# Decoding from the old states in the heads, and updating the states under the feed-forward network

## The chip, the cores and the metric

One core of one Trainium2 chip runs the whole step. The metric is the device time of one execution in microseconds; lower is better.

## The reference

One inference step of a one-layer decoder with two parallel branches, mLSTM ("m") and retention ("r"), four heads each, key and value width 256, model width 1024. A prompt of 528 tokens (16 meta tokens and 512) and eight running sequences with one new token each go through the same weights. All data are float32. Per head and branch, for each of the eight sequences (decoding):

```
mLSTM:      C_new = w_c * C + w_s * k v^T        h ~ q . C_new   (also n_new, and a denominator)
retention:  S_new = gamma * S + k v^T / 16       o ~ q . S_new
```

Then a norm per head, gates, an output projection, a layer norm, a SwiGLU feed-forward network (width 2816) and a second layer norm. Outputs are the prompt's and the sequences' activations, the prompt's final states, and the updated states C, n, m, S of the eight sequences. C and S of all sequences and heads are 64 blocks of 256 x 256 floats, 256 KB each; every block is read, and every updated block written.

## The kernel before, in words

**The main stream.** All large products go through TensorE in three passes each (high x low, low x high, high x high part of a float32 split in two float32r numbers). Weights come in 154 units of 128 x 1024 (512 KB), loaded from `wall` by SP into three `raw` buffers (`load_units`, L157), split by ACT into `wH` and by DVE into `wL` (`split_units`, L164; three buffers each). `run_step` (L193) runs one unit: 8 contraction steps of 6 matmuls with 260 or 268 columns. In its middle it splits the unit two ahead and loads the one five ahead (`prep`, L189). PSUM of the main stream (`pp`) has two buffers; a unit's result is evacuated while the next unit runs.

**The quarters.** Every two contraction steps (12 matmuls) `run_step` calls `tick`, which resumes generators that stopped at a `yield`, and then `side(i)`. A unit so has four quarters. In the heads' stage, 4 heads x 20 units, `sched` holds for each quarter 0 to 79 of a head (higher numbers run on into the next head) the side work due there: transposes, scores, value products, rotary embedding, norms, decoding. It is written out by hand in L966 to L1062. Engines work through their own queues in program order, so a side operation that waits holds back everything behind it on its engine, weight splits and evacuations too. Side products on TensorE use PSUM tiles `aux` and `acc`, two buffers each.

**Decoding before.** `dec_rows` (L814, at quarter 27 for m, 54 for r) transposes the eight sequences' q and k columns (L818), and POOL writes them to DRAM as 32 rows `kq` of 128 (L823). For each sequence `dec_load` (L832) has SP load the state block into `dC` (three buffers, L835) and one sequence's k and q rows, broadcast over all partitions in four pieces of 512 bytes, into `dkq` (three buffers, L838). `dec_unit` (L841) does this: two products k times v on ACT, a quarter later the new state on DVE, its store by POOL (L850), and two products of q with the new state, summed, on DVE:

```
act(t[:, et, :], k[:, 256:512], AF.Copy, scale=d["vs" + br][:, et, b:b + 1])
...
stt(c, c, w, t.rearrange("p a b -> p (a b)"), ALU.mult, ALU.add)
G.dma_start(o["dC" if br == "m" else "dS"][h, :, b, :], c)
...
stt(t[:, et, :], c[:, et * 256:(et + 1) * 256], 1.0, k[:, 0:256], ALU.mult, ALU.mult,
```

The units of a branch are due at the quarters in `DEC` (L976), their loads up to five quarters earlier. `dec_stat1` (L855, DVE: `pk`), `dec_stat2` (L872, a product with `ones` on TensorE, L877) and `dec_stat3` (L897) make the norm of the result, at 60, 62, 65 for m, 87, 89, 92 for r (the next head's 7, 9, 12), and 79, 82, 85 for r of the last head. `merge_a`, `merge_b` and `last_dec` use it.

**After the heads.** The output projection runs as eight `run_pair` calls (L220: two units, one half of 260 tokens), its first inputs reloaded into `mg`. The feed-forward network starts with four pairs for each token half (L1306 to L1313, eight units whose splits are kept), then 18 x 2 units (L1315), then the down projection (L1336, six columns of three units, then the last two columns in pairs). Side work: evacuations, weight splits, the first layer norm's second half during the first four pairs; POOL is idle from 695 us on until the last layer norm. `kv_load` (L670) reloads saved operands of one head's prompt state before the down projection, for products at the very end.

Of the kernel before, what the change touches and what calls it, by code (L numbers as in the profile page):

```python
# [19 lines left out]
T = 528  # L20
NB = 8
# [56 lines left out]
def body(nc, tc, a, o):  # L78
# [65 lines left out]
    onesR = const.tile([128, 2], F32R, name="onesR")  # L144
    nhalf = const.tile([128, 8], F32, name="nhalf")
# [121 lines left out]
    dsc = keep.tile([128, 3, H, NB], F32, name="dsc")  # L267
# [252 lines left out]

    def dcols(h, sec, r):
        d = tiles[h]
        br = sec[0]
        if sec[1] == "v":
            d["dc" + br] = sm.tile([128, 3, 2, NB], F32, name="dc")
        V.tensor_copy(d["dc" + br][:, "qkv".index(sec[1])], r[:, :, T:])
# [286 lines left out]

    def dec_rows(h, br):  # L814
        d = tiles[h]
        dc = d["dc" + br]
        ps = aux()
        PE.transpose(ps[:32, :128], dc[:, 0:2].rearrange("p s t b -> p (s t b)"), ident)  # L818
        t = wt("tmp", [128, NT], 3)[:32, :128]
        act(t, ps[:32, :128])  # L820
        kq = dram.tile([32, 128], F32, name="kq%d%s" % (h, br))
        d["kq" + br] = kq
        G.dma_start(kq, t)  # L823
        vs = sm.tile([128, 2, NB], F32, name="vs")
        if br == "m":
            tt(vs, dc[:, 2], dsc[:, 1, h:h + 1, :].to_broadcast([128, 2, NB]), ALU.mult, G)
        else:
            G.tensor_scalar(vs, dc[:, 2], 1.0 / 16, None, op0=ALU.mult)
        d["vs" + br] = vs
        d["y" + br] = sm.tile([128, 2, NB], F32, name="y")  # L830

    def dec_load(h, br, b):  # L832
        d = tiles[h]
        c = lt("dC", [128, 512], 3)
        SP.dma_start(c, a["sC" if br == "m" else "sS"][h, :, b, :])  # L835
        k = lt("dkq", [128, 512], 3)
        row = d["kq" + br].rearrange("(s b) c -> b s c", b=NB)[b:b + 1]
        SP.dma_start(k.rearrange("p (s c) -> p s c", s=4), row.broadcast_to([128, 4, 128]))  # L838
        d["dC" + br, b] = (c, k)

    def dec_unit(h, br, b):  # L841
        d = tiles[h]
        c, k = d["dC" + br, b]
# [4 lines left out]
        w = dsc[:, 0, h, b:b + 1] if br == "m" else float(GAMMA[h])  # L848
        stt(c, c, w, t.rearrange("p a b -> p (a b)"), ALU.mult, ALU.add)
        G.dma_start(o["dC" if br == "m" else "dS"][h, :, b, :], c)  # L850
        for et in range(2):
# [741 lines left out]
```

## Time and profile before

| | us |
|---|---|
| median of 3 runs (lowest, highest) | 1065.99 (1061.45, 1079.36) |
| the profiled execution's own time | 1068.46 |
| its span, first to last instruction | 1066.8 |
| heads' stage, to the last projection matmul | about 615 |
| matmuls of the 18 x 2 units of the network | 714 to 921 |
| down projection from | 921 |

Busy shares of the span: PE 97%, PE's weight loads 96%, DVE 56%, ACT 44%, POOL 17%. PE is TensorE, DVE VectorE, ACT ScalarE, POOL GpSimd, SP the engine that issues most loads. A row of the page's last part names an instruction group as line, engine, operation, output <- inputs. The granted clock is a share of TensorE's full 2.4 GHz.

### The profile page before, as it was taken

The numbers are of one execution on the slowest core, as the hardware profiler recorded it, in microseconds if no ns is written. First come the engines' busy times: TensorE is split into PE (matmuls) and PEld (weight loads), VectorE is DVE, ScalarE is ACT, GpSimd is POOL, SyncE is SP. The second block draws the span as 40 slices with busy tenths as digits, with TensorE's granted clock in tenths as the row PEclk, the third lists the DMA queues.
The fourth block names the chain that finished last, engine by engine and source line by source line (L and its number), as shares of the span: only waits on it lengthen the run. The fifth ranks groups of instructions, "written<-read, shape, count | busy, mean of one in ns | idle before, by whom it ended". The sixth has DMA issues, their size and how long they took to land.

```text
span 1066.8 us, 21079 instructions
## 1 busy us (share of the span) xinstructions
PE 1038.9 (97%) x8526; PEld 1028.3 (96%) x8526; DVE 595.4 (56%) x1236; ACT 467.2 (44%) x922; POOL 182.5 (17%) x313
## 2 busy tenths in 40 slices
PE   9999999999999999999998899999999999999996
PEld 8999998999999999999998899999999999999995
DVE  4748764568755487654596566734344343333435
ACT  5555553665544665545564434522222222222213
POOL 1223222322311232221122224200000000000003
PEclk9999999999999999999999899999999999999998
DMA  7254564555663645652456592212222222522302
GB/s 233 94 172 144 191 213 167 176 182 167 199 213 103 209 156 196 219 186 99 152 165 200 194 314 85 81 43 97 99 84 96 99 80 100 184 100 99 139 2 91
DMA packets 86249, 155.31 MB, mean 146 GB/s; under 512 B 8388, under 2 KB 49412, under 8 KB 85896
## 3 DMA queue, kind: packets, MB, share of 16 engines
q1 hardware_dynamic: 76904, 129.41, 36.9%
q0 software_dynamic: 9248, 24.56, 6.5%
q8 instruction: 67, 1.10, 0.4%
q14 instruction: 30, 0.25, 0.1%
HBM read 127.04 MB, written 25.58 MB: 143 GB/s over the span
## 4 chain that ended last, share of the span: by engine, by line
PE 71%; DMA 11%; DVE 8%; issue 5%; ACT 2%; POOL 1%; SPq 1%; ACTq 0%; DVEq 0%; POOLq 0%
PE pp L213 52%; PE pp L236 9%; DMA dkq<-kq3r 3%; DVE dC L100 1%; DMA dS<-dC 1%; PE aux L577 1%; DVE wL L97 1%; PE acc L177 1%; PE acc L178 1%; PE acc L179 1%; DVE dt L100 1%; DMA dkq<-kq0r 1%; DMA dkq<-kq2r 1%; PE pp L344 1%; DMA kq2r<-tmp 1%
## 5 line engine op out<-in xcount | busy, mean ns | idle before, releaser
L213 PE MATMUL pp<-xH,wL 128*128 128x260 f32 (+1 forms) x1248 | 262.9, 292 | 3.9 <-DVE sg L100 3.3
L213 PE MATMUL pp<-xL,wH 128*128 128x260 f32 (+1 forms) x1248 | 255.3, 286 | 0.0
L213 PE MATMUL pp<-xH,wH 128*128 128x260 f32 (+1 forms) x1248 | 254.9, 286 | 0.0
L97 DVE TENSOR_TENSOR wL<-raw,wH 128x1024 fp32r<-128x1024 f32 (+1 forms) x149 | 184.2, 1236 | 95.5 <-ACT wH L94 93.7
L213 PEld LDWEIGHTS pp<-xH,wL 128*128 128x128 f32 x1248 | 195.1, 191 | 5.5 <-DVE sg L100 3.8
L213 PEld LDWEIGHTS pp<-xH,wH 128*128 128x128 f32 x1248 | 195.7, 191 | 0.0
L213 PEld LDWEIGHTS pp<-xL,wH 128*128 128x128 f32 x1248 | 195.6, 191 | 0.0
L94 ACT ACTIVATE wH<-raw 128x1024 fp32r<-128x1024 f32 (+1 forms) x149 | 151.1, 1016 | 73.2 <-PE pp L213 58.3
L213 PE MATMUL pp<-x1H,wH 128*128 128x260 f32 x576 | 116.1, 283 | 0.0
L213 PE MATMUL pp<-x1L,wH 128*128 128x260 f32 x576 | 115.9, 283 | 0.0
L213 PE MATMUL pp<-x1H,wL 128*128 128x260 f32 x576 | 115.9, 282 | 0.0
L97 DVE TENSOR_TENSOR gt<-gt,pp 128x520 f32<-128x520 f32 (+1 forms) x52 | 31.8, 612 | 116.7 <-ACT gt L94 64.1
L213 PEld LDWEIGHTS pp<-x1H,wL 128*128 128x128 f32 x576 | 88.8, 188 | 0.0
L213 PEld LDWEIGHTS pp<-x1H,wH 128*128 128x128 f32 x576 | 88.8, 188 | 0.0
L213 PEld LDWEIGHTS pp<-x1L,wH 128*128 128x128 f32 x576 | 88.5, 188 | 0.0
L94 ACT ACTIVATE dt<-dkq,vs 128x256 f32<-128x256 f32 x128 | 57.8, 500 | 65.7 <-DMA dkq<-kq3r 21.8
L97 POOL TENSOR_TENSOR sq<-sq 128x260 f32<-128x260 f32 x12 | 9.2, 764 | 351.3 <-ACT sq L94 350.7
L94 ACT ACTIVATE hH<-gt 128x520 fp32r<-128x520 f32 (+1 forms) x26 | 14.9, 571 | 96.9 <-DVE gt L97 96.9
L213 PE MATMUL pp<-hH,wL 128*128 128x260 f32 x264 | 53.2, 283 | 0.0
L213 PE MATMUL pp<-hH,wH 128*128 128x260 f32 x264 | 53.1, 282 | 0.0
L213 PE MATMUL pp<-hL,wH 128*128 128x260 f32 x264 | 53.0, 282 | 0.0
L94 ACT ACTIVATE gt<-pp 128x520 f32<-128x520 f32 (+2 forms) x28 | 14.7, 526 | 81.9 <-PE pp L213 62.4
(371 smaller groups left out, 1927.9 us busy)
## 6 DMA issues: line engine op xcount, KB each, us to landing
raw<-wall SPq DMA_DIRECT2D x154, 512.0 KB, 3.5
dC<-sC SPq DMA_DIRECT2D x32, 256.0 KB, 4.9
dC<-dC POOLq DMA_DIRECT2D x32, 256.0 KB, 4.0
dC<-sS SPq DMA_DIRECT2D x32, 256.0 KB, 4.3
dS<-dC POOLq DMA_DIRECT2D x32, 256.0 KB, 4.0
raw<-xT SPq DMA_DIRECT2D x8, 268.0 KB, 4.6
mg<-mgd SPq DMA_DIRECT2D x8, 260.0 KB, 5.4
z<-xT SPq DMA_DIRECT2D x8, 260.0 KB, 6.4
```

The source lines that it names most:

```text
L94: A.activation(out, in_, func, **kw)
L97: (eng or V).tensor_tensor(out, x, y, op=op)
L100: V.scalar_tensor_tensor(out, x, s, y, op0=op0, op1=op1, **kw)
L177: PE.matmul(out, ll, rh, start=start, stop=False)
L178: PE.matmul(out, lh, rl, start=False, stop=False)
L179: PE.matmul(out, lh, rh, start=False, stop=stop)
L213: PE.matmul(ps[:, hi, :wd], w, r[:, lo:lo + wd], start=(st.first and i == 0 and pi == 0), stop=(st.last and i == n - 1 and pi == 2))
L236: PE.matmul(ps[:, hi, :n], w[:, c], r, start=(i == 0 and pi == 0), stop=(i == last and pi == 2))
L344: PE.matmul(first_ps[u][:, hi, :268], w[:, c], r[:, k, hi * 268:(hi + 1) * 268], start=(k == 0 and pi == 0), stop=(k == 7 and pi == 2))
L577: PE.transpose(ps[:m, i * 256 + dt * 128:i * 256 + dt * 128 + 128], src[:, dt, 128 * j:128 * j + m], ident)
```

## The change

Decoding no longer computes q . C_new from the updated block. It uses q . C_new = w_c (q . C) + w_s (q . k) v: two DVE products per block on the old state, and one small correction per branch, with q . k summed over partitions by a product with `ones` on TensorE. The rows go to DRAM as four rows of 1024, so that one broadcast load brings q for four sequences. The updated blocks are made again later: from the second token half of the network's first pairs on, POOL loads every block a second time (five buffers `uC`) with k rows for two sequences (`uk`), ACT and DVE compute the update, POOL stores it. `upd_at` starts an update every 13/4 quarters. `dsc` moves from pool `keep` to `const`, where `vsA` keeps the scaled v of all heads. Due times of decoding move, `kv_load` moves to the sixth down-projection column, and the SBUF space kept for POOL's DMA descriptors is set to 8192 bytes per partition.

```
+    dsc = const.tile([128, 3, H, NB], F32, name="dsc")
+    vsA = const.tile([128, 2 * H, 2, NB], F32, name="vsA")
...
+    kqd = {}
     def dec_rows(h, br):
         d = tiles[h]
         dc = d["dc" + br]
+        kp = sm.tile([128, NB, 2], F32, name="kp")
+        ks = sm.tile([128, NB], F32, name="ks")
+        tt(kp, dc[:, 0], dc[:, 1], ALU.mult, G)
+        tt(ks, kp[:, :, 0], kp[:, :, 1], ALU.add, G)
+        vs = vsA[:, 2 * h + (br == "r")]
+        v = dcol(h, br, 2)
+        if br == "m":
+            tt(vs, v, dsc[:, 1, h:h + 1, :].to_broadcast([128, 2, NB]), ALU.mult, G)
+        else:
+            G.tensor_scalar(vs, v, 1.0 / 16, None, op0=ALU.mult)
+        yield
         ps = aux()
-        PE.transpose(ps[:32, :128], dc[:, 0:2].rearrange("p s t b -> p (s t b)"), ident)
+        PE.transpose(ps[:32, :128], dc[:, 0:2].rearrange("p s b t -> p (s b t)"), ident)
+        PE.matmul(ps[:, 128:128 + NB], ones, ks, start=True, stop=True)
         t = wt("tmp", [128, NT], 3)[:32, :128]
         act(t, ps[:32, :128])
-        kq = dram.tile([32, 128], F32, name="kq%d%s" % (h, br))
-        G.dma_start(kq, t)
+        kq = dram.tile([4, 1024], F32, name="kq%d%s" % (h, br))
+        kqd[h, br] = kq
+        G.dma_start(kq.rearrange("a (r c) -> (a r) c", c=128), t)
+        vk = sm.tile([128, 2, NB], F32, name="vk")
+        tt(vk, vs, ps[:, 128:128 + NB]....to_broadcast([128, 2, NB]), ALU.mult)
...
     def dec_load(h, br, b):
         d = tiles[h]
-        c = lt("dC", [128, 512], 3)
+        if b % 4 == 0:
+            d["q4"] = lt("dq", [128, 1024], 2)
+            SP.dma_start(d["q4"], kqd[h, br][b // 4:b // 4 + 1, :].to_broadcast([128, 1024]))
+        c = lt("dC", [128, 512], 4)
         SP.dma_start(c, a["sC" if br == "m" else "sS"][h, :, b, :])
-        k = lt("dkq", [128, 512], 3)
-        row = d["kq" + br].rearrange("(s b) c -> b s c", b=NB)[b:b + 1]
-        SP.dma_start(k.rearrange("p (s c) -> p s c", s=4), row.broadcast_to([128, 4, 128]))
...
     def dec_unit(h, br, b):
         d = tiles[h]
-        t = lt("dt", [128, 2, 256], 2)
+        c, q = d["dC" + br, b]
+        t = lt("dt", [128, 256], 1)
         for et in range(2):
-            act(t[:, et, :], k[:, 256:512], AF.Copy, scale=d["vs" + br][:, et, b:b + 1])
-        yield
-        stt(c, c, w, t.rearrange("p a b -> p (a b)"), ALU.mult, ALU.add)
-        G.dma_start(o["dC" if br == "m" else "dS"][h, :, b, :], c)
+            stt(t, c[:, et * 256:(et + 1) * 256], 1.0, q, ALU.mult, ALU.mult, accum_out=d["y" + br][:, et, b:b + 1])

     def dec_stat1(h, br):
+        if br == "m":
+            tt(y, y, dsc[:, 0, h:h + 1, :].to_broadcast([128, 2, NB]), ALU.mult)
+            tt(y, y, d["vkm"], ALU.add)
+        else:
+            stt(y, y, float(GAMMA[h]), d["vkr"], ALU.mult, ALU.add)
...
-    DEC = {"m": (33, 35, 37, 42, 47, 52, 56, 59), "r": (64, 67, 70, 73, 76, 79, 82, 85),
-           "last": (58, 60, 62, 64, 66, 68, 70, 72)}
+    DEC = {"m": (35, 37, 39, 42, 45, 48, 51, 54), "r": (58, 61, 64, 67, 70, 73, 76, 79),
+           "last": (57, 59, 61, 63, 65, 67, 69, 71)}
-    DROW = {"m": 27, "r": 54}
+    DROW = {"m": 28, "r": 53}
...
-            at(h, DROW[br], P(dec_rows))
+            at(h, DROW[br] + late0 // 2, P(dec_rows))
-                at(h, max(tb - 5, DROW[br] + 1), P(dec_load, b))
+                at(h, max(tb - 5, DROW[br] + 2 + late0 // 2), P(dec_load, b))
-                e1, e2, e3 = 60, 62, 65
+                e1, e2, e3 = 56, 58, 61
-                e1, e2, e3 = 87, 89, 92
+                e1, e2, e3 = 81, 83, 86
-                e1, e2, e3 = 79, 82, 85
+                e1, e2, e3 = 73, 75, 78
...
+    dqp = tc.alloc_tile_pool(name="dq", bufs=1, side="right")
+    UPD = [(h, br, b) for h in range(H) for br in "mr" for b in range(NB)]
+    def upd_load(n):
+        if n < len(UPD):
+            h, br, b = UPD[n]
+            if b % 2 == 0:
+                upd["k"] = dqp.tile([128, 512], F32, name="uk", bufs=2)
+                r = 2 + b // 4
+                G.dma_start(upd["k"], kqd[h, br][r:r + 1, b % 4 * 256:b % 4 * 256 + 512].to_broadcast([128, 512]))
+            c = dqp.tile([128, 512], F32, name="uC", bufs=5)
+            G.dma_start(c, a["sC" if br == "m" else "sS"][h, :, b, :])
+            upd[n] = (c, upd["k"][:, b % 2 * 256:b % 2 * 256 + 256])
+    def upd_run(n):
+        h, br, b = UPD[n]
+        c, k = upd.pop(n)
+        t = [bt.tile([128, 260], F32, name="sq", bufs=8)[:, :256] for _ in range(2)]
+        for et in range(2):
+            act(t[et], k, AF.Copy, scale=vsA[:, 2 * h + (br == "r"), et, b:b + 1])
+        yield
+        w = dsc[:, 0, h, b:b + 1] if br == "m" else float(GAMMA[h])
+        for et in range(2):
+            x = c[:, et * 256:et * 256 + 256]
+            stt(x, x, w, t[et], ALU.mult, ALU.add)
+        G.dma_start(o["dC" if br == "m" else "dS"][h, :, b, :], c)
+        upd_load(n + 3)
+    UPQ = 13
+    def upd_at(i):
+        n = upd["n"]
+        if n < len(UPD) and 4 * upd["q"] >= UPQ * n:
+            start(upd_run(n))
+            upd["n"] += 1
+        upd["q"] += 1
...
     for lo in (0, 260):
+        if lo:
+            for n in range(3):
+                upd_load(n)
-            run_pair(ks, rhs_x1, lo, 260, ev_gu(i, lo), side if lo == 0 else None)
+            run_pair(ks, rhs_x1, lo, 260, ev_gu(i, lo), side if lo == 0 else upd_at)
...
-    kvp = tc.alloc_tile_pool(name="kvp", bufs=1)
-    kvx = kv_load(kvp)
     for j in range(6):
+        if j == 5:
+            assert upd["n"] == len(UPD) and not pending
+            dqp.release()
+            kvp = tc.alloc_tile_pool(name="kvp", bufs=1)
+            kvx = kv_load(kvp)
...
+    nc = _bacc.Bacc("TRN2", target_bir_lowering=False, num_devices=1, dynamic_dma_scratch_size=8192)
```

The 18 x 2 units and the six down-projection columns also get `upd_at` as their `side`.

## Rows read from the trace of the kernel before

**Rows 1.** The page: busy time, granted clock and GB/s in 40 slices.
```profile
PE 1038.9 (97%) x8526; PEld 1028.3 (96%) x8526; DVE 595.4 (56%) x1236; ACT 467.2 (44%) x922; POOL 182.5 (17%) x313
...
PEclk9999999999999999999999899999999999999998
...
GB/s 233 94 172 144 191 213 167 176 182 167 199 213 103 209 156 196 219 186 99 152 165 200 194 314 85 81 43 97 99 84 96 99 80 100 184 100 99 139 2 91
```

**Rows 2.** Waits of PE: waiter, who ended them, total us, times, longest.
```profile
PE aux L877 <- DVE pk L97: 5.4, 3, 2.0
PE acc L767 <- ACT dt L94: 3.7, 1, 3.7
PE pp L213 <- DVE sg L100: 3.3, 1, 3.3
```

**Rows 3.** Windows around PE's holes, and one of head 1 without.
```profile
core 0: us, PE busy (x) PEld busy (x) DVE busy (x) ACT busy (x) POOL busy (x), PEclk, DMA share, GB/s
171.00:179.90 8.90, 7.22 (x46) 7.01 (x47) 4.93 (x12) 3.64 (x6) 2.01 (x5) 0.81 0.60 204
316.90:326.10 9.20, 7.19 (x49) 6.97 (x47) 4.92 (x12) 3.90 (x6) 2.02 (x5) 0.81 0.47 165
466.40:473.80 7.40, 5.74 (x48) 5.52 (x47) 4.92 (x12) 3.65 (x6) 2.02 (x5) 1.00 0.66 215
568.20:583.50 15.30, 11.57 (x87) 11.09 (x83) 9.17 (x35) 9.52 (x27) 2.60 (x8) 0.89 0.56 177
593.50:609.70 16.20, 12.44 (x79) 11.79 (x78) 11.06 (x29) 6.29 (x12) 3.66 (x6) 0.79 0.55 192
...
271.40:281.00 9.60, 9.60 (x87) 9.60 (x84) 5.59 (x23) 5.33 (x18) 1.59 (x6) 1.00 0.70 216
```

**Rows 4.** The chain that ended last, start us and us, of 156:176 and 557:608.
```profile
158.46 2.42 DMA dS<-dC
...
161.28 9.29 DMA dkq<-kq0r
...
174.37 0.39 PE aux L877 x2
...
564.40 5.71 DMA dkq<-kq3r
```

**Rows 5.** Instructions that use tile dkq: duration ns least, median, most, and landing times.
```profile
L94 ACT ACTIVATE dt<-dkq,vs x128: 492/497/513, 71.1 to 609.6; 128x256 f32<-128x256 f32 x128
L100 DVE SCALAR_TENSOR_TENSOR dt<-dC,dkq x128: 417/423/428, 73.5 to 611.2; 128x256 f32<-128x256 f32 x128
L100 DVE DVE_READ_ACCUMULATOR dt<-dC,dkq x128: 79/81/84, 73.9 to 611.6; 128x1 f32 x128
...
DMA to landing us min/median/max: 4.9/6.7/9.9
```

**Rows 6.** DMA issues of the page: KB each, median us to landing.
```profile
raw<-wall SPq DMA_DIRECT2D x154, 512.0 KB, 3.5
```

**Rows 7.** The stores of kq (L823), eight of them: least, median, most.
```profile
DMA to landing us min/median/max: 3.6/7.4/8.4
```

**Rows 8.** Timelines of SP (550:575) and PE (555:569): start us, us.
```profile
558.58 0.33 SPq L161 DMA_DIRECT2D raw<-wall  x1
...
561.79 0.45 PE L213 MATMUL pp<-xH,wL 128*128 128x260 f32 x2
```

**Rows 9.** Timeline of PE, 423.3 to 426.2.
```profile
424.70 0.29 PE L877 MATMUL aux<-pk,ones 128*128 128x16 f32 x2
424.84 0.37 PE L177 MATMUL acc<-sH,qL 128*128 128x256 f32 x1
```

**Rows 10.** A window of the network's 18 x 2 units, columns as in rows 3.
```profile
714.00:921.00 207.00, 207.00 (x1725) 207.00 (x1724) 81.67 (x91) 56.72 (x73) 0.00 (x0) 1.00 0.26 91
```

**Rows 11.** POOL's stores of updated states (L850): ns, and us to landing.
```profile
L850 POOL DMA_DIRECT2D dC<-dC x32: 539/588/646, 74.1 to 575.6; - x32
...
DMA to landing us min/median/max: 2.3/4.0/8.8
```

More of the change, by code (lines that the diff above doesn't have):

```diff
@@ L519, in ev_raw, with dcol @@
         return go
+    def dcol(h, br, i):
+        return tiles[h]["dc" + br][:, i].rearrange("p b t -> p t b")
     def dcols(h, sec, r):
@@ L524, in dcols @@
         if sec[1] == "v":
-            d["dc" + br] = sm.tile([128, 3, 2, NB], F32, name="dc")
-        V.tensor_copy(d["dc" + br][:, "qkv".index(sec[1])], r[:, :, T:])
+            d["dc" + br] = sm.tile([128, 3, NB, 2], F32, name="dc")
+        V.tensor_copy(dcol(h, br, "qkv".index(sec[1])), r[:, :, T:])
     def rotary(h, sec, part):
@@ L833, in dec_load @@
         d = tiles[h]
[L834 removed]
+        if b % 4 == 0:
+            d["q4"] = lt("dq", [128, 1024], 2)
+            SP.dma_start(d["q4"], kqd[h, br][b // 4:b // 4 + 1, :].to_broadcast([128, 1024]))
+        c = lt("dC", [128, 512], 4)
         SP.dma_start(c, a["sC" if br == "m" else "sS"][h, :, b, :])
[L836 to L839 removed]
+        d["dC" + br, b] = (c, d["q4"][:, b % 4 * 256:b % 4 * 256 + 256])
     def dec_unit(h, br, b):
         d = tiles[h]
[L843 to L844 removed]
+        c, q = d["dC" + br, b]
+        t = lt("dt", [128, 256], 1)
         for et in range(2):
[L846 to L853 removed]
+            stt(t, c[:, et * 256:(et + 1) * 256], 1.0, q, ALU.mult, ALU.mult, accum_out=d["y" + br][:, et, b:b + 1])
     def dec_stat1(h, br):
@@ L860, in dec_stat1 @@
         if br == "m":
-            dc = d["dcm"]
             n1 = sm.tile([128, 2, NB], F32, name="n1")
@@ L864, in dec_stat1 @@
             ws = dsc[:, 1, h:h + 1, :].to_broadcast([128, 2, NB])
-            tt(n1, dc[:, 1], ws, ALU.mult)
+            tt(n1, dcol(h, "m", 1), ws, ALU.mult)
             tt(nst[:, h], nst[:, h], wc, ALU.mult)
             tt(nst[:, h], nst[:, h], n1, ALU.add)
-            tt(n1, nst[:, h], dc[:, 0], ALU.mult)
+            tt(n1, nst[:, h], dcol(h, "m", 0), ALU.mult)
             tt(pk[:, 1], n1[:, 0], n1[:, 1], ALU.add)
@@ L1262, in body @@
     full = [(0, 260), (260, 260)]
+    dqp = tc.alloc_tile_pool(name="dq", bufs=1, side="right")
+    UPD = [(h, br, b) for h in range(H) for br in "mr" for b in range(NB)]
+    upd = {"q": 0, "n": 0}
+    def upd_load(n):
[28 more added lines that the diff above has]
+        upd["q"] += 1
     NP = 4
@@ L1312, in body @@
                 load_units(UF + 2 * NP + i + 3)
-            run_pair(ks, rhs_x1, lo, 260, ev_gu(i, lo), side if lo == 0 else None)
+            run_pair(ks, rhs_x1, lo, 260, ev_gu(i, lo), side if lo == 0 else upd_at)
     unit = UF + 2 * NP
     for i in range(NP, FF):
-        run_step(Step(unit, kcols, rhs_x1, full, True, True, ev_g(i)))
-        run_step(Step(unit + 1, kcols, rhs_x1, full, True, True, ev_u(i)))
+        run_step(Step(unit, kcols, rhs_x1, full, True, True, ev_g(i)), upd_at)
+        run_step(Step(unit + 1, kcols, rhs_x1, full, True, True, ev_u(i)), upd_at)
         unit += 2
@@ L1339, in body @@
             ks = [(k0 + i, slice(i * 128, (i + 1) * 128)) for i in range(n)]
-            run_step(Step(unit, ks, rhs_h, full, k0 == 0, n == 6, ev_d(j)))
+            run_step(Step(unit, ks, rhs_h, full, k0 == 0, n == 6, ev_d(j)), upd_at)
             k0 += n
```

13 lines of the change are left out of this document (2 added, 11 removed).

## Prediction

> **What bounds the kernel now.** I read the page's busy times first: PE is busy 97% of the span, and its granted clock is close to full nearly everywhere [rows 1]. So only PE's holes count: the time in which it stands still, and the time after, when its clock is at the lower of its two levels (1.2 instead of 2.4 GHz). Look in the rows for two things: who ended PE's waits, and what the same stretch takes in a head without the wait.
>
> PE's waits come second. Between the start and the output projection three kinds are long: `dec_stat2` waiting for `pk`, three times, up to 2.0 us; a retention `pv` (L767) held by ACT's `dt`, 3.7 us; and a projection held by DVE's `sg`, 3.3 us [rows 2]. Third, I cut out the stretches around them [rows 3]. Idle is length minus PE busy: 8.90 - 7.22 = 1.68, 9.20 - 7.19 = 2.01, 7.40 - 5.74 = 1.66, 15.30 - 11.57 = 3.73 and 16.20 - 12.44 = 3.76, together 12.8 us. The first three are the turn from one head to the next, the last two lie in the last head. In four of the five the granted clock is below 1: after these holes PE ran at 1.2 GHz for a while. That costs length times missing clock: 8.90 x 0.19 = 1.69, 9.20 x 0.19 = 1.75, 15.30 x 0.11 = 1.68, 16.20 x 0.21 = 3.40, together 8.5, of which I put 0.5 on idle time, where it costs nothing. The holes cost 12.8 + 8.0 = 20.8 us. A check: the fourth stretch holds the same four quarters as 271.4 to 281.0 of head 1, which takes 9.60 with PE gapless; 15.30 - 9.60 = 5.7, against 3.73 + 1.68 = 5.4 by this account.
>
> Who is behind them? The chain of waits tells it at each of these places: a decode unit's ACT products wait for the broadcast rows `dkq`, which are issued only once a `dC` buffer has been stored, and take 5.7 to 9.3 us [rows 4]. Behind the waiting ACT stand evacuations and weight splits; behind DVE's waiting update stand `wL` and `pk`.
>
> **Part 1: decoding from the old state in the heads.** Per unit this removes two ACT products (497 ns each) [rows 5], the DVE update of 128 x 512, the store, and the wait for that store before `dC` is filled again. Two DVE products with their accumulator reads stay, 2 x (423 + 81) ns = 1.0 us [rows 5]. The broadcast becomes one of 512 KB for four units, in whole rows of 4 KB, where each unit had 256 KB in pieces of 512 bytes. The nearest rows: a weights load of 512 KB lands in 3.5 us [rows 6], a `dkq` of 256 KB in 6.7 [rows 5]. With four `dC` buffers, freed by DVE alone, and loads up to five quarters ahead, nothing in SP's queue waits for a store any more. The last retention unit is due at quarter 79 (71 in the last head) and its statistics start at 81 (73), so `pk`, late before, has slack. I take the whole 20.8 us away. Bounds: all of it, or only the turns between heads (1.68 + 2.01 + 1.66 + 1.69 + 1.75 = 8.8), if the last head keeps its holes. The saved ACT and DVE time as such is worth nothing: outside the holes neither is on PE's path.
>
> **What is late next.** The first unit of a branch still needs the `kq` rows by way of DRAM, and the engine that waits is now DVE. The tightest place is the first retention unit of the last head, due at quarter 57 (58 in the others). `dec_rows` starts at 53 with three small POOL operations; its PE part comes at the start of 54, ahead of the key-value products, so POOL can issue `kq` near 555.1, with no `dC` store ahead of it. It lands 3.6 us later at best, 7.4 at the median, 8.4 at worst [rows 7]. The slow ones had decode loads and stores in the queues before them, which are gone, so I take 3.6: 558.7. SP must also get past a weights load that waits for a split (issued at 558.58) [rows 8]; it issues the broadcast at 559.0. With that weights load just ahead I take 3.5 + 1.5 = 5 us for it; bounds 3.5 and the slowest `dkq`, 9.9 [rows 5]. So it lands at 564 (562.5 to 569), and the unit's `dC` load, issued behind it, some 0.6 later. Quarter 57 starts at 561.79 [rows 8]: DVE stands 2 to 3 us. Queued behind it are the low halves of scores, the two `yc` of the other branch's `dec_stat2` (due at 58) and a `wL`. PE needs that statistic's PSUM back for the scores of 59, near 565.5. DVE gets there at 564.6 + 1.0 for the unit + 0.9 for what follows = 566.5, so PE loses 1 us; bounds 0 and 5, and a low clock after the latter. In the other heads the unit comes after that statistic, and PE's next need is two quarters later: 0, bounds 0 and 4 each. SP's wait for `kq` delays no weights, since the next load is due only after quarter 58's split.
>
> `dec_rows` also gives PE a product of `ones` with eight columns. The nearest row is the statistic's product, after which the next matmul starts 0.14 us later (424.70, 424.84) [rows 9]. Eight of them: 1.1 us; bounds 0 and 3 (0.39 us each, as in the chain [rows 4]). It waits for POOL's `ks`, a quarter old by then. The tiny DVE additions in `dec_stat1` and `vk` lie in DVE's idle time.
>
> **Part 2: the updates under the feed-forward network.** There 1725 matmuls take 207 us, 120 ns each [rows 10]; a quarter of 12 is 1.44 us, and an update comes every 3.25 quarters, 4.68 us. 64 take 300 us. They begin with the second token half of the first pairs, 16 quarters before 714, at about 691, and end about 991, inside the network. In each 4.68 us come two ACT products, 0.99 us, on top of ACT's 27% (56.72 of 207): 48%; and two DVE updates like the 423 ns row, 0.85 us, on top of 39%: 57%. In the gapless stretch of head 1 these were 56% and 58% [rows 3]. PE stays covered, as a weight split starts a unit and a half (8.6 us) before its use. If that cover were gone, an update would cost up to 0.99 us, 63 us in all.
>
> DMA: 256 KB in, 256 KB out and 128 KB of rows per update, 655 kB in 4.68 us = 140 GB/s, on top of 91 [rows 10]: 231, against a slice of 314 on the page [rows 1]. POOL issues 64 stores, 64 loads and 32 row loads, 160 x 588 ns = 94 us of 300 [rows 11]. The load for update n + 3 is issued when n is done, 3 x 4.68 - 1.44 = 12.6 us ahead of its use; POOL's `dC` stores landed in 4.0 us, 8.8 at worst [rows 11]. POOL's new waits (for DVE's update, for an older store) have only further updates behind them. The first update alone is loaded as it starts: ACT waits some 0.6 + 4.0 us once, with `hH`, a split and an evacuation behind it. The pairs of that time use weights already split, so I take 0.5 us; bounds 0 and 3.
>
> `kv_load` moves to the last single down-projection column, still over 40 us ahead of its use: 0, bounds 0 and 3. The halved descriptor space for POOL's DMAs has no row; only a few are in flight at a time, so 0, bounds 0 and 5.
>
> **Sum.** 1068.46 (the profiled execution: span 1066.80 and 1.66 around it) - 20.8 + 1.0 + 1.1 + 0.5 = 1050.3. That execution lies 2.5 above the median 1065.99 of the runs shown (1061.45 to 1079.36); I credit half of that: 1049.0, 1.6% below the median. A measurement of this kernel tells about 2% from no change: faster means below 1044.7, slower above 1087.3.
>
> **Rivals.**
> A. No new wait at all, and the kernel before pays more than in this profile when it is measured again: 1065.99 - 21.5 = 1044.5. For: holes that open and close explain its scatter up to 1079. Against: this profile's own floor is 1068.46 - 20.8 = 1047.7. Chance 0.22.
> B. The last head keeps its holes in another form, at two thirds of 3.73 + 1.68 + 3.76 + 3.40 = 12.6: 1049 + 8 = 1057. For: its due times are the tightest. Against: no store and no ACT product is left in them. Chance 0.17.
> C. Slower than before: the first retention unit is late in all four heads. With the worst rows, `kq` 8.4 and broadcast 9.9, 18.3 us. The last head has 565.5 - 1.9 - 555.1 = 8.5 before PE stands, so it loses 9.8, the others, with two quarters of 2.4 us more, 5.0 each; each adds 1.7 for the clock: 11.5 + 3 x 6.7 = 31.6, less the 1 counted: 1079.6. It decides from 14.9 us on: there the four losses take back the whole gain of 17. Against: nothing large is queued ahead any more. Chance 0.06.
> D. The network starves: at the 165 GB/s of the slowest stretch [rows 3], 42 MB of updates and 30 MB of weights take 436 us instead of some 325: 1160. For: ACT and DVE wait in order. Against: the slice of 314. Chance 0.03.
> E. POOL becomes the bound: 160 issues in 300 us allow 1.87 us each. Were each held as long as a store's landing, 4.0 us, it would be 640 us: 1390. Against: 588 ns beside a DVE that was 58% busy. Chance 0.02. The Trainium skill, "SBUF — State Buffer", section "A bandwidth-pool intuition that's wrong (but worth ruling out)", speaks for this one: a POOL DMA of about 620 ns is said to take about 3100 beside a vector operation that holds the shared port, since its descriptors can't be written meanwhile. By that the estimate is 496 us for 160 issues and a time near 1245; the row of 588 ns does not show it here.
> The forecast has 0.50.
>
> Range: 1043 to 1062 leaves out C, D, E and the outer ends of A and B, about 0.2. Faster 0.23 (A and a little of the forecast), within 2% 0.72, slower 0.05 (D and E).
>
> **What would show it.** Right: no PE wait for `pk` at the turns and none for `dt`; granted clock 1.00 from 30 to 1050 us; `kq` landing near 3.6 us; PE gapless under the updates, with DVE near 57%, ACT near 48% and DMA near 231 GB/s. Wrong: DVE waiting for the `dq` broadcast at quarters 57 or 58 with PE idle behind it; ACT waiting for `uk`, or PE for `wL`, in the network; POOL issues over 1.87 us.

## The result, and the profile after

| | us |
|---|---|
| before, measured beside it: median of 4 runs (lowest, highest) | 1066.78 (1061.45, 1079.36) |
| after: median of 4 runs (lowest, highest) | 1049.91 (1049.27, 1051.18) |
| ratio, with its 95% interval | 0.9858 [0.9834, 0.9882] |
| predicted | 1049.0 (1043 to 1062) |
| the profiled execution: before, after | 1068.46, 1051.18 |

The kernel is 1.4% faster; the interval leaves out 1, and the gain is less than the 2% that the prediction asks for before it says faster. The time is the one forecast to 0.9 us; three of the terms behind it are not, and together they nearly cancel. The page of the kernel after, lines as in [rows 1]:

```profile
PE 1032.9 (98%) x8542; PEld 1024.5 (98%) x8542; DVE 602.2 (57%) x1320; ACT 465.3 (44%) x922; POOL 244.5 (23%) x425
...
PEclk9999999999999999999999999999999999999998
...
GB/s 240 92 143 142 138 143 94 170 154 130 163 107 97 202 139 145 157 95 74 132 147 192 139 227 103 97 236 227 226 245 239 225 246 233 226 239 221 216 23 92
```

Work of DVE and ACT and bytes have moved from the heads to the network (slices 27 to 38 carry some 230 GB/s where most of them carried 80 to 100). The busy totals of DVE and ACT are nearly what they were; the bytes grew, since every block is read twice. PE is what counts: 6.0 us less busy, and 17.3 us less span.

Where the 17.3 us lie is read from the same five stages cut out of both traces, each from its first TensorE matmul to that of the next: what precedes the heads, the heads, the output projection, the network's first part, the down projection and the end. Windows of the kernel before, columns as in [rows 3]:

```profile
0.00:22.74 22.74, 20.37 (x142) 18.96 (x143) 9.91 (x21) 11.21 (x22) 2.92 (x16) 1.00 0.81 269
22.74:615.54 592.80, 578.75 (x4724) 572.61 (x4723) 386.47 (x917) 319.73 (x686) 140.90 (x250) 0.99 0.53 172
615.54:666.39 50.85, 49.41 (x407) 48.25 (x406) 32.46 (x62) 21.09 (x37) 17.41 (x22) 1.00 0.57 200
666.39:921.84 255.45, 255.45 (x2131) 255.03 (x2130) 109.61 (x147) 78.42 (x121) 8.87 (x12) 1.00 0.25 88
921.84:1066.80 144.96, 134.90 (x1130) 133.48 (x1128) 56.96 (x90) 36.80 (x58) 12.41 (x15) 0.97 0.30 102
```

The same stages of the kernel after, and under them four stretches that are spoken of below:

```profile
0.00:21.93 21.93, 20.57 (x143) 19.60 (x143) 9.82 (x21) 11.14 (x22) 2.93 (x16) 1.00 0.82 279
21.93:598.74 576.81, 572.79 (x4744) 568.50 (x4743) 346.79 (x879) 266.93 (x558) 119.01 (x205) 1.00 0.40 135
598.74:648.34 49.60, 48.85 (x403) 47.74 (x402) 32.26 (x56) 21.05 (x37) 15.42 (x19) 1.00 0.52 181
648.34:904.65 256.31, 255.74 (x2132) 255.12 (x2130) 145.52 (x245) 117.31 (x218) 77.02 (x138) 1.00 0.68 215
904.65:1049.50 144.85, 134.94 (x1130) 133.52 (x1128) 67.82 (x120) 48.89 (x88) 30.17 (x48) 0.98 0.50 167
...
106.00:122.00 16.00, 14.03 (x105) 13.65 (x104) 10.78 (x33) 6.27 (x13) 2.75 (x6) 0.89 0.39 133
...
676.00:692.00 16.00, 15.43 (x129) 15.22 (x128) 9.26 (x21) 7.96 (x18) 7.48 (x14) 1.00 0.58 189
714.00:921.00 207.00, 207.00 (x1726) 207.00 (x1725) 112.05 (x176) 91.89 (x161) 59.00 (x110) 1.00 0.74 233
...
1028.00:1049.50 21.50, 11.59 (x102) 10.46 (x100) 12.85 (x33) 10.02 (x27) 8.94 (x11) 0.88 0.33 113
```

Line by line, the first number behind the edges: -0.8, -16.0, -1.25, +0.9, -0.1. The gain is the heads'. Before, they held 14.05 us without PE work (592.80 - 578.75), after, 4.02 (576.81 - 572.79), and PE's own time fell by 6.0, because less of it ran at the low clock. The network pays 0.9 for the updates. What PE still waits for in the kernel after (columns as in [rows 2]; waits that both kernels have are left out):

```profile
PE aux L838 <- POOL ks L97: 2.4, 4, 0.6
PE aux L837 <- DVE dc L531: 1.4, 1, 1.4
...
PE pp L239 <- DVE gt L97: 0.6, 1, 0.6
...
PE aux L180 <- ACT dn L94: 0.2, 1, 0.2
```

`pk`, `dt` and `sg`, the three of [rows 2], are gone. All but the third line here are new waits in the heads; the third is the start of the updates, at 685 us.

### The profile page after: what moved, and what is told of

Same layout as the page of the kernel before. It is cut to its first block, busy times and chain, and to the rows that moved or that the text cites. A ratio compares the mean times of both kernels' runs of the same rounds, so it can differ in the third digit from the quotient of the medians.

```text
span 1049.5 us, 21228 instructions
## 1 busy us (share of the span) xinstructions
PE 1032.9 (98%) x8542; PEld 1024.5 (98%) x8542; DVE 602.2 (57%) x1320; ACT 465.3 (44%) x922; POOL 244.5 (23%) x425
## 4 chain that ended last, share of the span: by engine, by line
PE 87%; DVE 5%; DMA 3%; ACT 2%; issue 1%; POOL 1%; SPq 0%; ACTq 0%; DVEq 0%; POOLq 0%
PE pp L216 67%; PE pp L239 8%; PE acc L180 2%; DVE wL L97 2%; PE acc L182 1%; PE acc L181 1%; PE aux L582 1%; PE aux L180 1%; PE pp L346 1%; PE aux L182 1%; PE aux L181 1%; DMA mg<-mgd 1%; DVE dt L100 1%; DMA z<-xT 1%; PE aux L811 1%
## 5 line engine op out<-in xcount | busy, mean ns | idle before, releaser
L216 PE MATMUL pp<-xH,wL 128*128 128x260 f32 (+1 forms) x1248 | 259.8, 289 | 0.0
L216 PE MATMUL pp<-xL,wH 128*128 128x260 f32 (+1 forms) x1248 | 252.7, 284 | 0.0
L97 DVE TENSOR_TENSOR wL<-raw,wH 128x1024 fp32r<-128x1024 f32 (+1 forms) x149 | 179.2, 1203 | 88.4 <-ACT wH L94 88.1
L216 PEld LDWEIGHTS pp<-xH,wH 128*128 128x128 f32 x1248 | 193.2, 189 | 0.0
L216 PEld LDWEIGHTS pp<-xL,wH 128*128 128x128 f32 x1248 | 193.1, 188 | 0.0
L94 ACT ACTIVATE raw<-pp,cols 128x536 f32<-128x536 f32 (+1 forms) x48 | 33.7, 702 | 75.5 <-PE pp L216 70.6
L94 ACT ACTIVATE sq<-uk,vsA 128x256 f32<-128x256 f32 x128 | 57.2, 497 | 9.5 <-DMA uk<-kq0m 5.7
L100 DVE SCALAR_TENSOR_TENSOR dt<-dC,dq 128x256 f32<-128x256 f32 x128 | 57.5, 449 | 4.9 <-DMA dC<-sS 2.0
L94 ACT ACTIVATE tmp<-pp,cols 128x520 f32<-128x520 f32 (+1 forms) x25 | 16.9, 678 | 75.4 <-PE pp L216 75.4
```

What stands on the lines that cost most here:

```text
L94: A.activation(out, in_, func, **kw)
L97: (eng or V).tensor_tensor(out, x, y, op=op)
L100: V.scalar_tensor_tensor(out, x, s, y, op0=op0, op1=op1, **kw)
L216: PE.matmul(ps[:, hi, :wd], w, r[:, lo:lo + wd], start=(st.first and i == 0 and pi == 0), stop=(st.last and i == n - 1 and pi == 2))
```

## The experiments

Three questions were put. Which part of the change removes the holes? What do its own new costs come to? How wide is the cover under the network? Labels with b_ start from the kernel before, labels with a_ from the kernel after. A ratio is always to the kernel before, measured beside it on the same chip. Different experiments ran on different chips, so between them the ratios and their intervals are compared.

**The ring of buffers.** A `dC` buffer of the kernel before goes round like this: broadcast lands 6.7 us after its issue [rows 5], two ACT products 1.0, about a quarter until DVE's turn (1.8: 570.83 us for 320 quarters in b_both, below), the update 0.7, the store's issue 0.5 and its landing 4.0 [rows 11]: about 14.7 us, an estimate from these rows. In the last head units are two quarters apart, so three buffers give a turn 3 x 2 x 1.8 = 10.7 us; in the other heads, three quarters apart, 16.0 us. By this the last head can't keep up at all, and the others only while landings stay near their medians. Three edits each take one piece out.

b_bufs4: more buffers, everything else as before (the descriptor space is set to 8192 bytes to make room, as in the change):

```
-        c = lt("dC", [128, 512], 3)
+        c = lt("dC", [128, 512], 5)
-        k = lt("dkq", [128, 512], 3)
+        k = lt("dkq", [128, 512], 4)
...
+    nc = _bacc.Bacc("TRN2", target_bir_lowering=False, num_devices=1, dynamic_dma_scratch_size=8192)
```

> The kernel before with five dC and four dkq buffers instead of three and three, and the smaller descriptor space that makes room for them; all work stays. My theory: SP's waits for the stores of dC (36.9 + 15.0 us) go and with them most of the holes, 1049 to 1057. Theory of less work on ACT, DVE and the DMA engines: no gain, 1063 to 1070.

Measured: 1049.85 us (1048.11 to 1051.65), ratio 0.9842 [0.9817, 0.9866]. With five buffers the ring has 5 x 3.6 = 18 us a turn. SP no longer waits for a store; the broadcast lands no sooner (4.7/6.5/10.3 us). One large hole is left, in the last head, in the view of PE's waits:

```profile
PE acc L767 <- ACT dt L94: 4.0, 1, 4.0
```

The ring does not explain this one, since 18 us is more than 14.7. By the timelines POOL issues the last head's retention `kq` at 544.67, SP waits 4.2 us for it to land and issues the first broadcast at 553.47, and ACT can start on it only at 559.98. So the first unit's way through DRAM is a second limit beside the ring.

b_rows2k: the `kq` rows stored per sequence, so that a unit's broadcast is one piece of 2 KB per partition, not four of 512 bytes; `dc` is laid out to suit (`dv` holds v):

```
-        kq = dram.tile([32, 128], F32, name="kq%d%s" % (h, br))
+        kq = dram.tile([NB, 512], F32, name="kq%d%s" % (h, br))
...
-        row = d["kq" + br].rearrange("(s b) c -> b s c", b=NB)[b:b + 1]
-        SP.dma_start(k.rearrange("p (s c) -> p s c", s=4), row.broadcast_to([128, 4, 128]))
+        SP.dma_start(k, d["kq" + br][b:b + 1, :].to_broadcast([128, 512]))
```

> The kernel before, with q and k of one sequence in one DRAM row, so that each broadcast is written in pieces of 2 KB instead of 512 bytes; the same bytes, stores and due times. If the slow broadcast is a main part of the lateness: its median landing falls from 6.7 to about 4.5 us and the time to 1052 to 1060. If the wait for the store alone makes it late: under 4 us gained, 1063 to 1067. By due times alone: 1067.

Measured: 1050.03 us (1047.32 to 1053.59), ratio 0.9845 [0.981, 0.988]. The instructions of tile `dkq`, against 4.9/6.7/9.9 in [rows 5]:

```profile
L841 SPq DMA_DIRECT2D dkq<-kq3r x8: 377/411/1007, 551.5 to 584.6; - x8
...
DMA to landing us min/median/max: 3.1/5.0/7.6
```

The same 256 KB land 1.7 us sooner at the median; a fall to 4.5 was expected, and the gain is larger than expected (1052 to 1060). The eight loads of the last head's retention units span 33.1 us, 4.7 per unit: still not the 3.6 of the schedule, and SP still waits 27.4 us for stores between 540 and 600 us. The Trainium skill, "Perfetto Trace Analysis", section "DMA Optimizations", says that transfers under 2 KB carry a considerable overhead each; these two rows agree.

b_nostore: the line of the store is left out, so the updated states are not written at all.

```
-        G.dma_start(o["dC" if br == "m" else "dS"][h, :, b, :], c)
```

> The kernel before without the stores of the updated blocks (the 64 state outputs are left unwritten). My theory, that ACT is held by late broadcast rows because a dC buffer must first be stored: the loads go out earlier, most of the 20.8 us of holes goes, 1049 to 1056 us against about 1067. Rival, that the change gained by its earlier due times: no change, 1063 to 1070. Rival, that the gain comes from ACT and DVE having less to do: no change either, since both products and the update stay.

Measured: 1044.0 us (1041.7 to 1045.92), ratio 0.9788 [0.9757, 0.982], more than expected. The turn is 14.7 - 4.5 = 10.2 us, just under the 10.7 of the last head, and one hole of 1.0 is left (`pk`).

b_both: the longer rows and the additional buffers together.

> The kernel before with both small edits: broadcast rows in pieces of 2 KB, and five dC and four dkq buffers; all work, due times and stores as before. My theory (only the lateness of the rows costs time): the holes that each edit alone left, 4 to 5 us of idle and clock, go too: 1043 to 1047 us, below the kernel after. Rival (the decode work itself has to leave the heads to get below 1050): 1049 to 1051, as each edit alone.

Measured: 1043.62 us (1043.4 to 1044.7), ratio 0.9798 [0.9773, 0.9823]. Its heads, then the loads of its last retention units, in the view of the instructions of tile `dkq` from 540 to 600 us:

```profile
22.39:593.22 570.83, 569.51 (x4724) 565.44 (x4723) 388.89 (x920) 320.73 (x687) 138.57 (x250) 1.00 0.54 180
```

```profile
L841 SPq DMA_DIRECT2D dkq<-kq3r x8: 326/428/857, 551.7 to 577.3; - x8
...
DMA to landing us min/median/max: 5.1/6.0/7.3
```

25.6 us over seven steps is 3.66 per unit: the pace of the schedule, two quarters. The last stores of the kernel before, by its line L850 from 555 to 612 us, show the pace that it reached:

```profile
L850 POOL DMA_DIRECT2D dS<-dC x8: 539/542/615, 572.1 to 611.1; - x8
```

39.0 over seven is 5.57 per unit, and a turn of three buffers 16.7 us. With the 2 KB rows alone a turn is 3 x 4.7 = 14.1. The sum has 14.7 for the one and 1.7 less, 13.0, for the other: a little short both times, but the order is right, and both lie above the 10.7 that the schedule allows. What follows: the holes of [rows 3] came in the main from a ring that was slightly too slow. Loosened by buffers or by rows alone it gives 1.6% (b_bufs4, b_rows2k), about what the whole change gives; loosened by both it gives 2.0%, and beats the change (the two intervals do not overlap), with all ACT products, updates and stores still in the heads: ACT is busy 320.73 us there against 266.93, and PE gapless in the heads but for 1.3 us.

b_early: the kernel before with the due times of the change, which are up to six quarters earlier.

```
-    DEC = {"m": (33, 35, 37, 42, 47, 52, 56, 59), "r": (64, 67, 70, 73, 76, 79, 82, 85),
-           "last": (58, 60, 62, 64, 66, 68, 70, 72)}
+    DEC = {"m": (35, 37, 39, 42, 45, 48, 51, 54), "r": (58, 61, 64, 67, 70, 73, 76, 79),
+           "last": (57, 59, 61, 63, 65, 67, 69, 71)}
...
```

> The kernel before with the due times of units and statistics of the kernel after, all else as before. Theory of the due times: most of the gain, 1048 to 1055. My theory: the rows are as late as they were and only waited for earlier, no gain, 1064 to 1080, with ACT waits for dkq longer than before and PE holes further forward, at quarters 58 to 62 of each head.

Measured: 1088.56 us (1086.69 to 1090.48), ratio 1.0205 [1.0176, 1.0233]. PE's waits:

```profile
PE acc L177 <- DVE sL L97: 22.8, 4, 7.9
PE aux L877 <- DVE pk L97: 8.4, 1, 8.4
```

Neither theory had this: the time is over the 1080 of the second, and the holes lie elsewhere. The four waits of `sL`, one per head, come before the retention units. In head 0, from PE's timeline and the view of ACT's waits:

```profile
116.09 0.55 PE L177 MATMUL acc<-vH,kwL 128*128 128x258 f32 x1 [5.46 <-DVE sL L97]
...
ACT dt L94 <- DMA dkq<-kq0m: 7.3, 2, 6.0
ACT dt L94 <- DMA dkq<-kq0r: 2.2, 2, 1.9
```

At 116 us POOL has not yet issued the retention rows (119.88). What is late is the mLSTM rows: the last five mLSTM units are now three quarters apart, where they were three to five. ACT waits up to 6.0 us for them here (2.9 in the kernel before) and up to 1.9 for the retention rows (7.5 before); in the last head both are late (7.0 and 8.4). DVE's update waits for ACT's `dt` (38.4 us in all, 7.0 at the longest, in the view of DVE's waits), and the split `sL` stands behind it in DVE's queue. SP's waits for the stores of mLSTM blocks grow from 15.0 to 40.4 us. So it is the ring again, asked for a faster turn at another place: it makes the kernel before slower by 2%.

a_oldtimes: the kernel after with the due times of the kernel before (the edit above, backwards).

> The kernel after with the due times of units and statistics of the kernel before (the rows' own times as after). If the earlier due times carry the gain: back to 1060 to 1068. If they carry none because loads and units no longer wait for stores: 1047 to 1051; the one hole to look for is the statistic at the turn of the heads, at most 1 us each.

Measured: 1047.69 us (1046.31 to 1048.84), ratio 0.9834 [0.9803, 0.9864]. So the earlier times carry none of the change's gain; by the medians they even cost it 2 us, which the two intervals do not quite separate.

**The change's own costs.** a_noupd leaves the updates out, so the updated states are not written: no second load, no products, no store.

```
-            start(upd_run(n))
...
-            for n in range(3):
-                upd_load(n)
+            pass
```

> The kernel after without the 64 updates, their loads and their stores (the updated states are left unwritten). If the updates are hidden under the network but for the 0.6 us hole at their start: 1048 to 1050. Rival, that they slow the network by contention for SBUF, DMA or the clock: 1040 to 1046.

Measured: 1049.15 us (1048.39 to 1050.68), ratio 0.985 [0.9824, 0.9876]. 64 updates, with 42 MB and a fifth of ACT's time under the network (128 products of 0.5 us in 300), cost 0.8 us, and the intervals do not tell that from nothing.

a_ks: the product of `ones` with `ks` a quarter after the transposes, and head 0's retention rows a quarter later.

```
-        PE.matmul(ps[:, 128:128 + NB], ones, ks, start=True, stop=True)
...
         G.dma_start(kq.rearrange("a (r c) -> (a r) c", c=128), t)
+        yield
+        ps = aux()
+        PE.matmul(ps[:, 128:128 + NB], ones, ks, start=True, stop=True)
...
-            at(h, DROW[br] + late0 // 2, P(dec_rows))
+            lag = 1 if h == 0 and br == "r" else late0 // 2
+            at(h, DROW[br] + lag, P(dec_rows))
```

> The kernel after, with the product of ones and ks a quarter later than the transposes, and the first head's retention rows one quarter later. If PE's waits for ks (4 x 0.6 us) and for dc (1.4 us and some 1.7 us at the lower clock) cost what the trace shows: 5 us less, 1044 to 1046. Rival: the time moves to DVE's wait for the first retention unit, a quarter later now in the first head, or the products wait as before: 1049 to 1051.

Measured: 1049.26 us (1048.3 to 1051.14), ratio 0.9851 [0.9828, 0.9874]. Not the 1044 to 1046 that was expected of it; the time lies in the rival's range. Its heads and its last 21.6 us:

```profile
21.77:593.65 571.88, 570.32 (x4744) 566.85 (x4743) 346.56 (x879) 266.62 (x558) 118.01 (x205) 1.00 0.41 136
1025.00:1046.60 21.60, 11.73 (x85) 10.56 (x83) 10.86 (x28) 8.05 (x22) 7.42 (x9) 0.66 0.33 112
```

The heads are 4.9 us shorter (571.88 against 576.81), with no wait for `ks` or `dc`. But the last head has a hole of 1.3 us that was 0.2 (`aux` L180 behind ACT's `dn`, behind a DVE that waits 3.1 us for the state block), and the end runs at a mean clock of 0.66 where the kernel after has 0.88 over as long a stretch: from the product of `ones` with `z` to the last instruction it takes 17.25 us (1029.35 to 1046.60) against 15.09 (1034.41 to 1049.50). In the profiled pair 2.9 us of the 4.9 are left (spans of 1046.6 and 1049.5), in the medians 0.65. The pair flatters the edit: it sets 1051.18 us against 1048.30, where the medians are 1049.91 and 1049.26, and part of what the edit removes is in that one trace of the kernel after only, as the part on the failed step shows. How much of the small gain in the medians this explains was not measured.

a_best: the edit of a_ks, the due times of the kernel before, and the first three updates loaded two pairs before they start.

```
-        if lo:
-            for n in range(3):
-                upd_load(n)
...
+            if not lo and i == 2:
+                for n in range(3):
+                    upd_load(n)
```

> The changed kernel with three of its own new costs taken out at once: the product of ones with ks a quarter after the transposes, the due times of the kernel before, and the first three updates loaded two pairs before they start. The theory that the changed kernel is behind the kernel before with 2 KB rows and more buffers only by these: the four ks waits (2.4), the dc wait and its clock (1.4 + 1.7), the hole in the last head and the late first update (0.2 to 0.8 each) all go, and the time comes to 1043.0 to 1045.5, level with that kernel's 1043.6. The rival, that these holes only move (the low clock at the end took back what the ks edit gave when it was made alone): 1047 to 1049.5, with a stretch of low clock after 1030 us that is twice as long as in the kernel before.

Measured: 1043.26 us (1042.4 to 1045.05), ratio 0.9782 [0.975, 0.9814]: as the first theory had it, level with b_both. Its heads and its network:

```profile
22.46:591.84 569.38, 569.30 (x4740) 566.13 (x4739) 343.62 (x876) 268.06 (x559) 112.50 (x202) 1.00 0.41 137
640.16:895.62 255.46, 255.46 (x2131) 255.05 (x2130) 145.46 (x245) 117.46 (x219) 76.99 (x139) 1.00 0.68 216
```

Gapless to 0.1 us in the heads, and 255.46 us for the network with most of the updates in it (the rest run under the down projection), where the kernel before has 255.45 with none. The three costs together are 6.6 us (1049.91 - 1043.26). Of the two that were also taken out alone, one gave 0.65 (a_ks) and one 2.2 (a_oldtimes); the early loads were not tried alone. In a_ks a hole that was closed let the next one open (0.2 to 1.3 us); that this holds for the rest of the 6.6 is not shown.

b_best: b_both, with the mLSTM statistics one or two quarters later, after its last hole.

```
-                e1, e2, e3 = 60, 62, 65
+                e1, e2, e3 = 61, 64, 66
```

> The kernel before with 2 KB rows and more buffers, and the mLSTM statistics at quarters 61, 64 and 66 instead of 60, 62 and 65. If the one hole that is left (1.1 us, TensorE waiting for pk in the last head) is a matter of these due times, it goes, and the time comes to 1041.5 to 1043.0. If the hole cost no more than its idle time or moves to the merge behind it: 1043 to 1044.5.

Measured: 1047.09 us (1045.69 to 1048.4), ratio 0.9816 [0.9784, 0.9848]: 3.5 us above b_both, where no theory had it (on another chip; the intervals of the two ratios overlap). PE's waits:

```profile
PE pp L213 <- DVE sg L100: 1.6, 4, 0.4
PE acc L771 <- ACT dt L94: 1.3, 1, 1.3
```

The hole for `pk` shrank to 0.2, but the merge behind the statistics (`sg`) is now late in every head, and `dt` in the last. In this order the later quarters had no slack to take the statistics.

**How wide the cover is.** a_pace8 and a_pace5 set the distance of the updates, 13/4 quarters (4.68 us) in the change, to 8/4 (2.88 us) and 5/4 (1.80 us): `UPQ = 8`, `UPQ = 5`.

> The changed kernel with an update every 8/4 quarters (2.88 us) instead of 13/4 (4.68). Three loads ahead are then 3 x 2.88 - 1.44 = 7.2 us against landings of 5.6 to 6.1; some 319 GB/s. If the cover is as wide as predicted, ScalarE waits for uk a few times and TensorE stays gapless: 1049 to 1053. If the network or the issues of GpSimd bound the updates already near the even pace: ScalarE waits at most updates, TensorE idles behind the weight splits, over 1060.

> The changed kernel with an update every 5/4 quarters (1.8 us): loads 3 x 1.8 - 1.44 = 4.0 us ahead, less than the 5.6 to 6.1 that they take to land, and some 455 GB/s. The theory that the even pace is what hides the updates: ScalarE waits for uC's k rows and VectorE for uC at most updates, TensorE loses 10 to 40 us behind them, 1060 to 1090. The rival, that the updates would be hidden at any pace, since the weights are split a unit and a half ahead: 1049 to 1052.

Measured: 1054.8 us (1052.23 to 1055.74), ratio 0.9885 [0.9845, 0.9926], and 1116.75 us (1111.23 to 1118.5), ratio 1.047 [1.0421, 1.0519]. At 8/4, DVE's updates (first for mLSTM, then for retention; first and last start) and a window of the network:

```profile
L100 DVE SCALAR_TENSOR_TENSOR uC<-uC,dsc,sq x64: 476/480/486, 679.8 to 840.9; 128x256 f32<-128x256 f32 x64
L100 DVE SCALAR_TENSOR_TENSOR uC<-uC,sq x64: 414/419/429, 701.3 to 864.4; 128x256 f32<-128x256 f32 x64
```

```profile
690.00:870.00 180.00, 175.89 (x1451) 174.66 (x1452) 111.71 (x200) 96.26 (x184) 77.90 (x146) 1.00 0.88 303
```

The same at 5/4:

```profile
L100 DVE SCALAR_TENSOR_TENSOR uC<-uC,dsc,sq x64: 473/479/486, 679.5 to 831.4; 128x256 f32<-128x256 f32 x64
L100 DVE SCALAR_TENSOR_TENSOR uC<-uC,sq x64: 414/419/427, 703.4 to 853.9; 128x256 f32<-128x256 f32 x64
```

```profile
690.00:870.00 180.00, 140.84 (x1008) 137.54 (x1007) 93.37 (x178) 83.75 (x166) 77.55 (x146) 0.89 0.81 278
```

From the first start to the last, 64 updates took 864.4 - 679.8 = 184.6 us in the one and 174.4 in the other, 2.9 and 2.8 us each, though the second asked for 1.8. So at 5/4 this ring (load three ahead, update, store) gives an update every 2.8 us and no faster. Asked for 2.88 it already loses 4.1 us of PE in this window; asked for 1.8, PE follows the ring: 180.00 - 140.84 = 39.2 us idle and 11% of the clock, 20 us, about the 60 by which its profiled execution is longer (1111.23 against 1051.18). The theory of the even pace had the sign of this and too small a size (10 to 40 us); at 8/4 the time falls between its two cases. The cover of the change ends somewhere between 4.68 us an update, where it holds, and 2.88, where it does not; no run lies between. What sets the 2.8 us was not separated. The rows lean to the round trip of three loads: at 5/4 the blocks land in 5.8 (mLSTM) and 5.5 us (retention) at the median, about as in the change (5.6 and 6.1), and the 278 GB/s are less than the 303 of 8/4.

## Why the prediction was right, and where it was not

**What bounds it and who is behind the holes: right.** The four edits that loosen the ring (b_bufs4, b_rows2k, b_both) or leave the store out (b_nostore) removed all or most of the holes and ended between 1043.6 and 1050.0. In the profiled execution of the kernel after the granted clock is full but for a stretch at 112 us and the end. That decoding from the old states is needed for this would not be true: two more `dC` buffers and one more `dkq` do as much (0.9842 against 0.9858).

**The size of the holes: 2.5 us too small.** Predicted 20.8. The heads of a_best take 569.4 us, those of b_both without their one hole 569.5 (PE busy), against 592.80: 23.3. The five windows of [rows 3] held 12.8 of the 14.05 us idle, and 8.0 was put on the clock where PE's busy time is 578.75 - 569.51 = 9.2 above the gapless one. The whole stage, cut against itself, would have given the first of these before the change.

**"It waits for POOL's `ks`, a quarter old by then": the step that failed.** The kernel after at that place in head 1, and two other waits of this section, by the timeline (start us, us, idle time before and what ended it in brackets):

```profile
255.66 0.22 POOL L97 TENSOR_TENSOR kp<-dc 128x16 f32<-128x16 f32 x1 [12.20 <-DVE dc L531]
255.97 0.57 POOL L97 TENSOR_TENSOR ks<-kp 128x8 f32<-128x8 f32 x1
...
255.42 0.17 DVE L531 COPY dc<-raw 128x16 f32<-128x16 f32 x1
255.79 0.69 DVE L97 TENSOR_TENSOR qL<-raw,qH 128x512 fp32r<-128x512 f32 x1 [0.20 <-ACT qH L94]
...
255.73 0.27 PE L837 MATMUL aux<-ident,dc 128*32 128x128 f32 x1
256.59 0.39 PE L838 MATMUL aux<-ks,ones 128*128 128x8 f32 x2 [0.59 <-POOL ks L97]
...
559.41 0.43 DVE L100 SCALAR_TENSOR_TENSOR dt<-dC,dq 128x256 f32<-128x256 f32 x1 [2.04 <-DMA dC<-sS]
...
681.17 0.91 ACT L94 ACTIVATE sq<-uk,vsA 128x256 f32<-128x256 f32 x2 [4.49 <-DMA uk<-kq0m]
```

POOL's two operations were indeed first in its queue, a quarter earlier. They could not run: their input `dc` is a copy by DVE (L531), which came at 255.42, 0.3 us before PE's transposes. So PE stood 0.59 us in each head for `ks`, and in head 0, where the copy was later still, 1.38 for `dc`, after which the clock fell (the window of 106 to 122: 16.00 x 0.11 = 1.8). The prediction followed the queue of the engine that computes `ks` and not the engine that makes its input. Priced 0, it cost 2.4 + 1.4 + 1.8 = 5.6 in this execution. With the 0.2 of the last head the heads lie 576.81 - 569.38 = 7.4 above a_best's; 1.6 of that no row here names.

Two things limit this. Some 0.4 of the 0.59 us is not the late input: `ks` takes 0.57 us here and 0.20 in the mLSTM rows (in head 0 it is `kp` that takes 0.59), and ends just after the DVE product `qL` that runs beside it; no run separates this. And the 1.4 and 1.8 us are this execution's. a_noupd has the same program in its heads; its wait for `dc` is 0.3 us, and its heads and its window of 106 to 122 are

```profile
21.66:596.12 574.46, 571.41 (x4744) 567.12 (x4743) 346.01 (x879) 266.62 (x558) 119.23 (x205) 1.00 0.40 135
...
106.00:122.00 16.00, 15.08 (x126) 14.70 (x125) 10.96 (x38) 7.85 (x16) 5.04 (x12) 1.00 0.46 150
```

a_pace8 and a_pace5 are alike (0.3 us; heads of 574.83 and 574.03). In these three the step costs 2.6 to 2.7 us, and the heads lie 4.7 to 5.5 above a_best's.

**The first retention unit of the last head: the wait right, its price too high.** DVE was to stand 2 to 3 us: 2.04, in the timeline above, at 559.41. It waited for the state block and not for the broadcast, which lands in 5.0 us at the median, as taken. `kq` lands in 1.7 us at the median and not in 3.6. That the stores ahead of it are gone is not reason enough: in b_nostore, without them, it still takes 4.5. PE lost 0.2 and not 1.0; in a_ks the same wait is 1.3.

**Eight products with `ones`, 1.1: too high.** PE's busy time in the heads is 569.30 with them (a_best) and 569.51 without (b_both); no cost shows.

**The start of the updates, 0.5: right.** ACT waited 4.49 us where 4.6 was predicted, PE 0.57. a_best shows that it was not necessary.

**The updates under the network: right.** From 714 to 921 us (18 us further on in the work than the same stretch of the kernel before) PE is gapless, DVE busy 112.05 of 207 (54%, predicted 57), ACT 91.89 (44%, predicted 48), 233 GB/s (predicted 231).

**The sum.** Between the two profiled executions 18.2 us were predicted (20.8 - 1.0 - 1.1 - 0.5) and 17.3 measured: 2.5 more for the holes; 7.4 of new cost in the heads, not 2.1 (1.0 + 1.1), so 5.3 less; and outside the heads 1.3 gained where 0.5 was to be lost, 1.8 more, most of it in the output projection, which the prediction left out. That the total came out within 1 us is partly luck. So is the last step: half of 2.5 us was credited because the profiled execution of the kernel before lay that far above the median, and the profiled execution of the kernel after happened to lie 1.3 above its own.

**The rivals.** A's 1044.5 is what the change gives without its own waits (a_best, 1043.26); as it stands it has them, and the kernel before did not come out slower when it was measured again (1066.78). B: in the last head no hole came back beyond the 0.2 of `dn` and the 0.6 for `ks` that every head has. C: the first retention unit was late in the last head only, by 2.04 us; no run here made it late in all four. D: the network carried 233 GB/s with PE gapless. E: the instructions of tile `uC` on POOL, 32 each,

```profile
L1291 POOL DMA_DIRECT2D uC<-sC x32: 538/538/552, 677.8 to 918.7; - x32
L1305 POOL DMA_DIRECT2D dC<-uC x32: 547/547/549, 683.4 to 929.9; - x32
```

and the two groups for `sS` and `dS` never take over 0.56 us, beside a DVE that is busy 54%. The Trainium skill ("SBUF — State Buffer", "A bandwidth-pool intuition that's wrong (but worth ruling out)") measured its 3100 ns beside a DVE `tensor_copy`. From 677 to 971 us DVE ran only TENSOR_TENSOR and SCALAR_TENSOR_TENSOR here, so this kernel does not put that figure to the test.

## What to carry to other kernels

Where transfers go round a few buffers, add up one turn (load, each engine's part, the wait between them, store) and set it beside buffers times the distance of the units, before anything is restructured: here a few more buffers or a longer row were worth what a rewrite of the decoding was. An operand's age is that of its last input, so follow it back to the engine that makes it, not only to the queue that it stands in. Cut whole stages against a stretch without holes, and not only the holes that the list of waits shows.

## What was not expected of the hardware

The same 256 KB broadcast from DRAM to 128 partitions lands in 6.7 us as pieces of 512 bytes and in 5.0 us as pieces of 2 KB (medians of the kernel before and b_rows2k); with more buffers it is 6.5 and 5.6 (b_bufs4, b_both). The small `kq` store lands in 1.7 us in the kernel after and in 7.4 in the kernel before [rows 7]; without the state stores alone it is 4.5 (b_nostore), so what else is on the way counts too. The end of the program ran at mean clocks between 0.66 (a_ks) and 0.88 (the kernel after) over stretches of one length, behind the same wait of 0.6 us; a change elsewhere in a kernel can be hidden or feigned by 2 us in this way. One program can also differ between executions: the wait for `dc` in head 0 was 1.4 us with a low clock behind it in one trace, and 0.3 us with a full clock in three others of the same heads. A step read from one trace is worth a look at a second.
